# Feed-forward loops of a two-layer transformer block: each engine's order written out by unit of work

## The chip, the cores and the metric

The kernel runs on one core of one Trainium2 chip. A core has TensorE (PE in the profile, with PEld for its weight loads), VectorE (DVE), ScalarE (ACT), GpSimd (POOL) and SyncE (SP), which work through queues of their own and wait for one another by semaphores. Matmuls write to PSUM, which has 8 banks of 128 partitions x 512 fp32 words; everything else lies in SBUF. The metric is the device time of one execution in microseconds, lower is better. It was measured three times for the kernel before.

## The reference

A block of two layers over 512 image tokens and 256 context tokens, width 1024, in fp32. Layer 0 mixes the tokens by a gated part and a differential attention, layer 1 by an attention over a window. Each layer ends in a feed-forward, and the final output is normalised. What matters here (FFN_HIDDEN is 2816):

```python
def swiglu(h, w_in, w_out):
    g, u = jnp.split(h @ w_in, 2, axis=-1)
    return (jax.nn.silu(g) * u) @ w_out
...
mod = silu_c @ ada_w[l] + ada_b[l]
...
h = h + g2 * swiglu(modulate(h, norm2_g[l], sh2, sc2), ffn_w_in[l], ffn_w_out[l])
if need_ctx:
    hc = hc + cg2 * swiglu(modulate(hc, norm2_g[l], csh2, csc2), ffn_w_in[l], ffn_w_out[l])
```

`need_ctx` holds in layer 0 alone, so its feed-forward works on 768 tokens and that of layer 1 on 512. `mod` for layer 1 is a product of one vector with a 1024 x 6144 matrix (a second one, with `silu_cc`, for its first two parts).

## The kernel before

**Arithmetic.** Each fp32 product is made of three matmuls on the parts of a split (`mm3`): a value is rounded to fp32r by a cast on ScalarE (the high part), and the rest is a subtraction (the low part); then high x high, high x low and low x high are added up in PSUM. So each weight tile, 128 x 512, takes a cast on ScalarE (L913) and a subtraction on GpSimd or VectorE (L917).

**Feed-forward.** `ffn(l)` runs over 22 hidden tiles f of 128 columns. For one f the raw weights are one load of 1 MB, 128 x 2048: four quarters a11, a12 (gate, first and second half of the 1024 inputs), a21, a22 (up). With tokens in two halves of NH (384 in layer 0, 256 in layer 1) this is a 2 x 2 product of 2 x 2 blocks. The first two tiles (three in layer 1) do it directly, eight block products; those are needed while the second half of the tokens is still being prepared. From then on `product(n, f)` makes seven block products in the manner of Strassen and Winograd, numbered 1 to 7, 12 matmuls each (four of 128 inputs, three each). Four of their weights are sums that VectorE makes from the quarters: 5 = a21 + a22, 6 = that less a11, 3 = a12 less that, 7 = a11 less a21 (L968). 1, 2 and 4 use a11, a12 and a22. The accumulators are two banks (one `wide` tile) for each f: products 1, 6, 7, 4 add up in the first, 5 and 3 in the second, and product 2 has a bank of its own. Between them results are read out: after 1 VectorE adds the copy of product 2 (L996, L997) and ScalarE applies Silu; 6 is copied (L1001); 5 is copied to `u` (L1005); after 3 VectorE adds (L1008) and ScalarE applies Silu; after 7 VectorE adds to `u` (L1012) and multiplies (L1014); after 4 it multiplies again (L1017). As 6, 7 and 4 go on adding into the bank just read, each waits for that read. Then the gated tile `hs` is split into `hh` (L116 on ScalarE, L117 on GpSimd).

**Second layer.** A pair of hidden tiles g = (2g, 2g+1) with one of the 8 output tiles m is an output unit: 6 matmuls of 512 columns and, in layer 0, 6 of 256. Each writes one of three `pb` banks, and VectorE adds it to the residual (L766). Output units of a pair are put among the products of the two following hidden tiles. The order in the program is in strings; a digit is a product, a letter an output unit:

```python
("2156ab37cd4", "2a1b56c3d74", "2a1b56c3de7f4ghij", "2a1b56c3de7f4g")[f % 2 if f < NF - 1 else l + 2]
```

So on even f the order is 2156ab37cd4, on odd f 2a1b56c3d74 (for f = 3 each letter is two units). The letters from e on are units of the last pair of which only the first hidden tile is ready.

**Who orders.** The program is scheduled by the compiler's planner, which orders each engine's instructions by priority (program order) and a simulated time; a later instruction may be put ahead of an earlier one. `issue_after(ins)` makes what is created within it come after `ins` on the same engine, without a wait on the chip. The kernel before uses it at a few places only.

**Buffers.** Split weights: 8 tiles in layer 0 (tags `w` and `wf`), 12 in layer 1. Raw first-layer weights: two tiles, in layer 1 a third in the ring. Raw second-layer weights `rawo`: 128 x 1024, one tile in layer 0, two in layer 1. Sums: the two `t` tiles and `sumsq`. Split gated tiles `hh`: six, for three hidden tiles. All loads go out on SP's queue.

**Modulation of layer 1.** In `ffn(0)` the 48 tiles of `ada1` (128 x 1024) are loaded into two buffers (`ar`, L216) and multiplied with the broadcast vector on VectorE (L222, `junk`), the first 16 of them twice. `more` puts one tile after each of four steps of a hidden tile, from f = 4 on.

## Time and profile before

| | us |
|---|---|
| median of three runs | 1638.63 |
| lowest, highest | 1636.87, 1643.16 |
| the profiled execution, first to last instruction | 1641.9 |
| loop over f = 3 to 21 in `ffn(0)` with its end, about | 458 to 960 |
| the same in `ffn(1)`, about | 1288 to 1626 |

The time of the profiled execution beyond its span is not given by the profile; the span is 3.3 us above the median of the runs. In the rows below a matmul lasts longer than the distance to the next one, as matmuls are pipelined: the pace is read from starts, or from a busy stretch and its count. An entry in square brackets is the time in which the engine was idle before an instruction, and what ended it. In rows by group, the last columns are the busy time, the mean of one in ns, and the idle time before them.

### The profile page before, as it was taken

The page shows a single profiled execution, that of the slowest core. Times are in us where ns is not written, and L with a number is a line of the kernel's source. Part 1 is how long each engine was busy: PE and PEld are TensorE (multiplying, and loading weights), DVE is VectorE, ACT ScalarE, POOL GpSimd, SP SyncE. Part 2 cuts the span into 40 slices and gives each one's busy share as a digit, 9 for nine tenths or more (in the row PEclk, how much of TensorE's full clock was granted, in tenths as well). Part 3 has the DMA queues.
Part 4 walks back from the last instruction along what each step waited for, and adds up shares of the span by engine and source line. Part 5 has one row for each costly group of instructions (what it writes and reads, how often), then busy time and mean ns, then how long its engine had stood idle before and what let it go on. Part 6 is the DMA issues. An engine that isn't in the chain of part 4 may idle for free.

```text
span 1641.9 us, 24642 instructions
## 1 busy us (share of the span) xinstructions
PE 1542.8 (94%) x9547; PEld 1367.1 (83%) x9547; DVE 1073.0 (65%) x1980; ACT 724.5 (44%) x1472; POOL 766.9 (47%) x543
## 2 busy tenths in 40 slices
PE   6999989999999999999999988999989999999996
PEld 4776877899899889998989978777868989898886
DVE  4621788756857788666665585665667857666665
ACT  2423675645533233333333244555664544444443
POOL 0463221062157666666666316532222466675662
PEclk9999989999999999999999999999999999999998
DMA  8744100141223343343432012110233222322201
GB/s 317 298 153 169 40 7 1 65 139 68 76 79 116 105 139 131 105 150 126 142 131 77 27 51 91 52 33 25 74 116 123 65 103 92 101 90 103 90 27 52
DMA packets 47957, 161.98 MB, mean 99 GB/s; under 512 B 5472, under 2 KB 9952, under 8 KB 40160
## 3 DMA queue, kind: packets, MB, share of 16 engines
q1 hardware_dynamic: 47696, 160.28, 28.4%
q8 instruction: 75, 1.23, 0.3%
q14 instruction: 42, 0.34, 0.1%
q10 hardware_dynamic: 144, 0.13, 0.0%
HBM read 158.29 MB, written 2.10 MB: 98 GB/s over the span
## 4 chain that ended last, share of the span: by engine, by line
PE 69%; DVE 11%; POOL 6%; DMA 5%; ACT 4%; issue 3%; POOLq 0%; SPq 0%; DVEq 0%; ACTq 0%
PE pw L100 9%; PE pw L101 9%; PE pw L102 9%; PE pb L100 7%; PE pb L101 7%; PE pb L102 7%; POOL w L917 5%; DMA raw<-ffn_in 3%; PE pf L100 3%; PE pf L101 2%; PE pf L102 2%; PE pb L1257 2%; PE pb L1246 2%; PE pf L351 2%; DVE t L968 2%
## 5 line engine op out<-in xcount | busy, mean ns | idle before, releaser
L100 PE MATMUL pw<-ax,w 128*128 128x384 f32 (+2 forms) x732 | 237.5, 328 | 16.1 <-DVE q L1012 6.7
L101 PE MATMUL pw<-ax,w 128*128 128x384 f32 (+2 forms) x732 | 237.9, 325 | 4.1 <-DVE ax L458 2.5
L78 POOL TENSOR_TENSOR w<-raw,w 128x512 fp32r<-128x512 f32 (+1 forms) x84 | 127.6, 1526 | 243.2 <-ACT w L75 220.8
L102 PE MATMUL pw<-ax,w 128*128 128x384 f32 (+2 forms) x732 | 236.7, 325 | 2.1 <-POOL w L917 2.1
L917 POOL TENSOR_TENSOR w<-raw,w 128x512 fp32r<-128x512 f32 x119 | 177.7, 1507 | 54.2 <-ACT w L913 53.4
L917 POOL TENSOR_TENSOR w<-t,w 128x512 fp32r<-128x512 f32 x90 | 133.4, 1482 | 139.9 <-ACT w L913 136.5
L100 PE MATMUL pb<-hh,w 128*128 128x512 f32 x480 | 167.3, 362 | 12.8 <-ACT hh L116 8.3
L766 DVE SCALAR_TENSOR_TENSOR xT<-pb,mod,xT 128x512 f32<-128x512 f32 (+3 forms) x208 | 144.5, 704 | 43.8 <-PE pb L102 43.1
L101 PE MATMUL pb<-hh,w 128*128 128x512 f32 x480 | 171.2, 358 | 0.5 <-POOL hh L117 0.5
L102 PE MATMUL pb<-hh,w 128*128 128x512 f32 x480 | 170.7, 357 | 0.0
L100 PEld LDWEIGHTS pw<-ax,w 128*128 128x128 f32 x732 | 142.0, 195 | 27.2 <-DVE q L1012 8.1
L100 PE MATMUL pw<-T,w 128*128 128x384 f32 (+1 forms) x508 | 159.1, 314 | 4.8 <-DVE hs L1008 2.4
L101 PE MATMUL pw<-T,w 128*128 128x384 f32 (+1 forms) x508 | 158.6, 312 | 4.0 <-DVE T L117 4.0
L102 PE MATMUL pw<-T,w 128*128 128x384 f32 (+1 forms) x508 | 158.2, 312 | 0.0
L101 PEld LDWEIGHTS pw<-ax,w 128*128 128x128 f32 x732 | 142.6, 195 | 12.1 <-DVE ax L458 3.4
L102 PEld LDWEIGHTS pw<-ax,w 128*128 128x128 f32 x732 | 142.4, 195 | 6.0 <-POOL w L917 2.7
L913 ACT CAST w<-t 128x512 fp32r<-128x512 f32 x104 | 64.5, 621 | 176.8 <-DVE t L968 122.5
L917 POOL TENSOR_TENSOR w<-rawo,w 128x512 fp32r<-128x512 f32 x63 | 94.1, 1493 | 66.5 <-ACT w L913 66.5
L100 PEld LDWEIGHTS pb<-hh,w 128*128 128x128 f32 x480 | 89.5, 189 | 27.0 <-ACT hh L116 10.8
L100 PEld LDWEIGHTS pw<-T,w 128*128 128x128 f32 x508 | 97.2, 192 | 9.7 <-DVE hs L1008 3.9
L101 PEld LDWEIGHTS pw<-T,w 128*128 128x128 f32 x508 | 97.4, 192 | 6.6 <-DVE T L117 4.6
L102 PEld LDWEIGHTS pb<-hh,w 128*128 128x128 f32 x480 | 90.3, 188 | 13.1
(363 smaller groups left out, 4056.7 us busy)
## 6 DMA issues: line engine op xcount, KB each, us to landing
raw<-ffn_in SPq DMA_DIRECT2D x44, 1024.0 KB, 4.9
ar<-ada SPq DMA_DIRECT2D x24, 1024.0 KB, 7.3
ar<-ada SPq DMA_DIRECT2D x48, 512.0 KB, 3.5
rawo<-ffn_out SPq DMA_DIRECT2D x44, 512.0 KB, 3.9
raw<-odd_out SPq DMA_DIRECT2D x32, 256.0 KB, 2.7
raw<-qk SPq DMA_DIRECT2D x16, 256.0 KB, 7.9
raw<-uv SPq DMA_DIRECT2D x16, 256.0 KB, 2.7
raw<-even_out SPq DMA_DIRECT2D x8, 512.0 KB, 4.2
```

The lines of the kernel that those rows point to most:

```text
L78: eng.tensor_tensor(lo, raw, hi.bitcast(F32), ALU.subtract)
L100: mm(out, s[0], m[0], start=start, stop=False, **kw)
L101: mm(out, s[0], m[1], start=False, stop=False, **kw)
L102: return mm(out, s[1], m[0], start=False, stop=stop, **kw)
L351: nc.tensor.matmul(ps[32 * q:32 * q + 32, :w], cst[:, k, :], t[:, w * q:w * q + w], start=k == 0, stop=k == KT - 1, skip_group_check=True)
L766: self.nc.vector.scalar_tensor_tensor(h, ps[:, r], self.modcol(l, j, m, who), h, ALU.mult, ALU.add)
L913: nc.scalar.copy(t[:, 0, :], src)
L917: eng.tensor_tensor(t[:, 1, :], src, t[:, 0, :].bitcast(F32), ALU.subtract)
L968: nc.vector.tensor_tensor(t, x, y, how)
L1246: last = nc.tensor.transpose(pt[:, x * P:(x + 1) * P], es[2 * (x % 2) + x // 2][:, kb * P:(kb + 1) * P], self.ident)
L1257: nc.tensor.matmul(po[64 * h:64 * h + 64, :], V[vb][:, 64 * g:64 * g + 64], t[:, h * TC:h * TC + TC], start=kb == 0, stop=kb == nb - 1, sk ...
```

## The change

In `ffn` each engine's instructions of the loop are chained in the written order (`run`, one chain each for PE, DVE, ACT, POOL and SP). The order is a list of units; weights are prepared by a list of jobs in the order of their use, 8 (layer 0) or 12 (layer 1) ahead of the units. An output unit stands between most products: 215s6s3s7s4 for every f from 4 on. Each product pair of accumulators becomes two single banks out of four; for that the wide PSUM tiles move to a pool of their own, which is released and opened again around the feed-forwards. Product 2 uses the `fill` bank and is copied at once. Second-layer weights are loaded in tiles of 128 x 512, two in layer 0 and six in layer 1. The modulation tiles are loaded from ScalarE's queue, three for each hidden tile from f = 3 on, and their dots have three fixed places, after products 1 and 7 and after the second output unit. All low parts of weights go to GpSimd, but for one of two second-layer tiles in layer 1. The direct tiles and everything outside the feed-forwards keep their work. The diff, cut to its core:

```diff
     def wide(self):
-        return self.pp.tile([P, 1024], F32, name=self.uid("pw"), tag="w", bufs=2)
+        return self.wp.tile([P, 1024], F32, name=self.uid("pw"), tag="w", bufs=2)
+    def single(self):
+        return self.wp.tile([P, 512], F32, name=self.uid("pw"), tag="s", bufs=4)
+    def open_wide(self):
+        self.wp = self.tc.alloc_tile_pool(name=self.uid("wide"), bufs=1, space=bass.MemoryType.PSUM)
...
         self.close_ring()
+        self.wp.release()
+        self.open_wide()
...
+        tail, tiles = {}, []
+        def run(key, fn, *args, **kw):
+            with tc.issue_after(tail[key].ins) if key in tail else ExitStack():
+                tail[key] = fn(*args, **kw)
+            return tail[key]
+        def add(key, out, x, y, how):
+            return run(key, {"DVE": nc.vector, "POOL": nc.gpsimd}[key].tensor_tensor, out, x, y, how)
+        def ada_load():
+            if todo:
                 ll, j, k = todo.pop(0)
-                t = self.ada_tile(ll, j, k)
+                t = self.adap.tile([P, D], F32, name=self.uid("ar"), tag="ar", bufs=self.ada_bufs)
+                r = (j * KT + k) * P
+                run("ACT", nc.scalar.dma_start, t, a["ada1"][r:r + P, :])
+                tiles.append((ll, j, k, t))
+        def ada_dots():
+            if tiles:
+                ll, j, k, t = tiles.pop(0)
                 for who in range(2 if j < 2 else 1):
-                    self.ada_dot(ll, j, k, t, who)
+                    run("DVE", self.ada_dot, ll, j, k, t, who)
...
+        nrawo = (2, 6)[l]
+        halves = [(g, h) for g in range(NF // 2) for h in range(4)]
+        def load():
+            if halves:
+                g, h = halves.pop(0)
+                t = ring.tile([P, 512], F32, name=self.uid("rawo"), tag="rawo", bufs=nrawo)
+                run("SP", nc.sync.dma_start, t, a["ffn_out"][l, g, :, h * 512:h * 512 + 512])
+                outs.append(t)
...
-                w_ = self.wide()
-                state[f] = [w_[:, :NH], w_[:, 512:512 + NH]]
+                state[f] = [self.single()[:, :NH] for _ in range(2)]
...
+            for k in range(len(W)):
+                run("PE", self.mm3, ps, W[k], A[k], k == 0, k == len(W) - 1)
+            run("DVE", self.residual, l, 5, m, off, n, ps)
...
+            for v in ("2ss1s5s6s3s7s4s" if f == 3 else "215s6s3s7s4" if f < NF - 1 else
+                      ("215s6s3s7sef4ghij", "215s6s3s7sef4g")[l]):
+                if v.isdigit():
+                    units.append((int(v), f))
+                    jobs.append((int(v), f))
+                elif v == "s":
+                    g, m = todo_m.pop(0)
+                    units.append(("s", g, m))
+                    if m % 2 == 0:
+                        jobs.append(("s", g, m))
                 else:
-                    m = "efghijkl".index(v)
-                    Wl.append(s2_weights(NF // 2 - 1, m))
-                    for off, n in whos:
-                        s2_part((NF - 2,), m, Wl[m][:1], off, n)
-        ahead = len(Wl)
-        for m in range(ahead, KT):
-            Wl.append(s2_weights(NF // 2 - 1, m))
+                    units.append(("t", "efghij".index(v)))
+        jobs += [("b", m) for m in range(0, KT, 2)]
+        R = (8, 12)[l]
+        Wt, Wl, sumt = {}, [], []
+        def sum_tile():
+            self.ns += 1
+            sumt.append(self.sumsq()[:, :512] if self.ns % 3 == 2 else self.tmp("t"))
+            return sumt[-1]
+        self.ns = 0
+        ahead_raw = (2, 3)[l]
...
+        def sums(j):
+            n, f = j
+            if n in (5, 6, 3, 7):
+                r = raws[f]
+                a11, a12, a21, a22 = [r[:, i * 512:(i + 1) * 512] for i in range(4)]
+                old = sumt[-1] if sumt else None
+                x, y, how = {5: (a21, a22, ALU.add), 6: (old, a11, ALU.subtract), 3: (a12, old, ALU.subtract),
+                             7: (a11, a21, ALU.subtract)}[n]
+                due[j] = sum_tile()
+                add("DVE", due[j], x, y, how)
+        due, late = {}, []
+        def job():
+            if late:
+                add("DVE", *late.pop())
+            if len(jobs) > 1 and jobs[1][0] not in ("s", "b"):
+                sums(jobs[1])
+            if not jobs:
+                return
+            j = jobs.pop(0)
+            if j[0] == "s":
+                t = Wt[j] = wtile()
+                prepare(outs.pop(0), t, l == 1 and j[2] % 4 == 2)
+                load()
+            elif j[0] == "b":
+                m = j[1]
+                if m % 4 == 0:
+                    f = NF + m // 4
+                    pool = ring if l and f % 3 == 2 else self.Rf
+                    self.big = pool.tile([P, 2048], F32R, name=self.uid("raw"), tag="raw", bufs=1 if pool is ring else 2)
+                t = self.big[:, m % 4 * 512:m % 4 * 512 + 1024].rearrange("p (a b) -> p a b", a=2)
+                prepare(outs.pop(0), t)
+                load()
+                Wl.extend(pieces(t, i) for i in (m, m + 1))
+            else:
+                n, f = j
+                i = {1: 0, 2: 1, 4: 3}.get(n)
+                t = Wt[j] = wtile()
+                prepare(due.pop(j) if i is None else raws[f][:, i * 512:(i + 1) * 512], t)
+                if n == 4:
+                    del raws[f]
+                    if f + ahead_raw < NF:
+                        with tc.issue_after(tail["SP"].ins):
+                            raws[f + ahead_raw] = raw(f + ahead_raw)
+                        tail["SP"] = self.last_raw
+        def prepare(src, t, dve=False):
+            run("ACT", nc.scalar.copy, t[:, 0, :], src)
+            lo = t[:, 1, :], src, t[:, 0, :].bitcast(F32), ALU.subtract
+            if dve:
+                late.append(lo)
+            else:
+                add("POOL", *lo)
...
+            if n == 2:
+                out = st["p2"] = self.fill()[:, :NH]
+                g = st["g"] = self.gated_tile(ring if own else None)
+            elif n == 1:
+                st["w"] = [self.single()[:, :NH] for _ in range(2)]
+                out = st["w"][0]
+            else:
+                out = st["w"][n in (5, 3)]
+            for j in range(4):
+                c = slice(j * P, (j + 1) * P)
+                run("PE", self.mm3, out, (w[:, 0, c], w[:, 1, c]), op[n][j], j == 0 and n in (1, 2, 5), j == 3)
+            g = st["g"]
+            A, B = g[:, :NH], g[:, NH:]
+            ps0, ps1 = st.get("w", (None, None))
+            if n == 2:
+                run("ACT", nc.scalar.copy, A, out)
+            elif n == 1:
+                add("DVE", A, A, ps0, ALU.add)
+                run("ACT", nc.scalar.activation, A, A, AF.Silu)
+                ada_dots()
+            elif n == 6:
+                run("ACT", nc.scalar.copy, B, ps0)
+            elif n == 5:
+                st["u"] = ring.tile([P, NH], F32, name=self.uid("u"), tag="u", bufs=1) if own else self.tmp()[:, :NH]
+                run("ACT", nc.scalar.copy, st["u"], ps1)
+            elif n == 3:
+                add("DVE", B, B, ps1, ALU.add)
+                run("ACT", nc.scalar.activation, B, B, AF.Silu)
+            elif n == 7:
+                add("DVE", st["u"], st["u"], ps0, ALU.add)
+                add("DVE", B, B, st["u"], ALU.mult)
+                ada_dots()
+            else:
+                add("DVE", A, A, ps0, ALU.mult)
+                hi, lo = self.hidden(F32R), self.hidden(F32R)
+                parts = [slice(0, T)] if f < NF - 1 else [slice(NH, T), slice(0, NH)]
+                for c in parts:
+                    run("ACT", nc.scalar.copy, hi[:, c], g[:, c])
+                    add("POOL" if f < NF - 1 else "DVE", lo[:, c], g[:, c], hi[:, c].bitcast(F32), ALU.subtract)
+                hid.append((hi, lo))
+                del state[f]
...
+        with tc.issue_after(self.last_w.ins):
+            for f in range(3, 3 + ahead_raw):
+                raws[f] = raw(f)
+            for _ in range(nrawo):
+                load()
+        for _ in range(R):
+            job()
+        for u in units:
+            if u[0] == "s":
+                g, m = u[1:]
+                for off, n in whos:
+                    s2_part((2 * g, 2 * g + 1), m, pieces(Wt[("s", g, m // 2 * 2)], m), off, n, True)
+                if m % 4 == 1:
+                    ada_dots()
+                if m % 4 in (0, 2, 3) and (m < 4 or g):
+                    ada_load()
+                if m % 2 == 0:
+                    continue
+            elif u[0] == "t":
+                m = u[1]
+                for off, n in whos:
+                    s2_part((NF - 2,), m, Wl[m][:1], off, n, True)
+            else:
+                unit(*u)
+            job()
+        ahead = sum(u[0] == "t" for u in units)
+        while jobs:
+            job()
```

More of the change, by code (lines that the diff above doesn't have):

```diff
@@ L969, in weights @@
             return slot({1: a11, 2: a12, 4: a22}.get(n) if n in (1, 2, 4) else sums[f])
-        def more(n, f, ins):
-            if todo and n in (1, 3, 6, 7) and f >= 4:
-                with tc.issue_after(ins.ins):
-                    ada_some(1)
         def product(n, f):
@@ L1311, in final_rows @@
         dg = self.dg[:, off:off + n]
-        r = self.rstd_rows(sq[:, off:off + n], n, 1.0 / D, self.wide, dg, more, self.bank if off else self.fill)
+        r = self.rstd_rows(sq[:, off:off + n], n, 1.0 / D, self.single, dg, more, self.bank if off else self.fill)
         rs = self.p0.tile([P, 512], F32, name=self.uid("rs"), tag="tq"[off > 0], bufs=2)[:, :n]
```

67 lines of the change are left out of this document (24 added, 43 removed).

## The prediction

> **What bounds the kernel now.** I read the page first, then busy time by stretches, then who TensorE waited for in the two feed-forward loops, then the order of time around two of the waits.
>
> ```profile
> span 1641.9 us, 24642 instructions
> ...
> PE 1542.8 (94%) x9547; PEld 1367.1 (83%) x9547; DVE 1073.0 (65%) x1980; ACT 724.5 (44%) x1472; POOL 766.9 (47%) x543
> ...
> PE 69%; DVE 11%; POOL 6%; DMA 5%; ACT 4%; issue 3%; POOLq 0%; SPq 0%; DVEq 0%; ACTq 0%
> ```
>
> TensorE is busy 94% of the span, so no reordering can bring much; but the chain that ended last is only 69% TensorE. The stretches of the two loops (columns: stretch, its length, then busy us of PE, PEld, DVE, ACT, POOL with counts, granted clock, DMA share, GB/s):
>
> ```profile
> 458.00:960.00 502.00, 485.76 (x2739) 454.94 (x2738) 343.52 (x514) 170.41 (x309) 304.15 (x196) 0.99 0.33 110
> 1266.00:1626.00 360.00, 342.54 (x2325) 316.85 (x2326) 239.91 (x375) 163.13 (x350) 212.36 (x155) 0.98 0.23 77
> 520.00:580.00 60.00, 56.39 (x305) 52.79 (x303) 47.67 (x68) 18.91 (x34) 39.23 (x23) 0.94 0.37 124
> 580.00:630.00 50.00, 47.05 (x260) 43.35 (x261) 42.73 (x57) 16.56 (x31) 32.03 (x20) 1.00 0.37 117
> 630.00:680.00 50.00, 50.00 (x286) 47.12 (x285) 38.12 (x59) 18.59 (x34) 36.91 (x24) 1.00 0.42 141
> 1430.00:1465.00 35.00, 35.00 (x239) 32.42 (x238) 25.39 (x37) 16.07 (x34) 25.03 (x18) 1.00 0.35 121
> ```
>
> Undisturbed, a matmul of loop 0 takes 50.00/286 = 0.175 us and one of loop 1 35.00/239 = 0.146 us. A hidden tile has 84 product matmuls and 48 (loop 1: 24) for the second layer: 132 x 0.175 = 23.1 us and 108 x 0.146 = 15.8 us. Where TensorE did wait, in 470 to 946 us and in 1298 to 1616 us (total, times, longest):
>
> ```profile
> PE pb L100 <- ACT hh L116: 8.3, 6, 2.9
> PE pb L100 <- ACT hs L996: 4.1, 4, 1.6
> PE pw L100 <- ACT hs L1001: 1.8, 1, 1.8
> PE pb L100 <- DVE ctxT L766: 1.2, 2, 0.8
> ```
> ```profile
> PE pw L100 <- DVE q L1012: 6.7, 4, 2.5
> PE pw L100 <- DVE u L1012: 4.7, 2, 2.4
> PE pw L100 <- DVE hs L1008: 2.4, 4, 0.8
> PE pw L100 <- ACT u L1005: 0.8, 1, 0.8
> ```
>
> That is 8.3 + 4.1 + 1.8 + 1.2 = 15.4 us in loop 0 and 6.7 + 4.7 + 2.4 + 0.8 = 14.6 us in loop 1. Their cause shows in the order of time, once in each loop:
>
> ```profile
> 753.38 0.34 PE L102 MATMUL pw<-T,w 128*128 128x384 f32 x1
> 753.99 0.69 DVE L968 TENSOR_TENSOR t<-raw 128x512 f32<-128x512 f32 x1 [2.77 <-DMA raw<-ffn_in]
> 754.60 0.55 DVE L1017 TENSOR_TENSOR hs<-hs,pw 128x384 f32<-128x384 f32 x1
> 755.17 0.83 ACT L116 CAST hh<-hs 128x768 fp32r<-128x768 f32 x1 [2.89 <-DVE hs L1017]
> 756.06 0.50 PE L100 MATMUL pb<-hh,w 128*128 128x512 f32 x1 [2.35 <-ACT hh L116]
> ```
> ```profile
> 1348.60 0.28 PE L102 MATMUL pw<-T,w 128*128 128x256 f32 x1
> 1350.17 0.69 DVE L968 TENSOR_TENSOR t<-raw 128x512 f32<-128x512 f32 x1 [5.15 <-DMA raw<-ffn_in]
> 1350.78 0.41 DVE L1012 TENSOR_TENSOR u<-u,pw 128x256 f32<-128x256 f32 x1
> 1351.24 0.39 PE L100 MATMUL pw<-ax,w 128*128 128x256 f32 x1 [2.36 <-DVE u L1012]
> ```
>
> VectorE's order holds a weight sum of a later hidden tile (L968) ahead of a PSUM read that TensorE needs (L1017, L1012). The sum sits until its raw weights land, VectorE idle 2.77 and 5.15 us before it, and the read, the cast and TensorE stand behind it. The load had gone out only 7.5 us before the sum ran (1350.17 - 1342.64):
>
> ```profile
> 1342.64 0.33 SPq L804 DMA_DIRECT2D raw<-ffn_in  x1
> ```
>
> **The change, part by part.** *Raw weights and sums.* Sums become jobs in the order of use, 8 or 12 tiles ahead and no further; the next raw load goes out when the last quarter (a22) of a tile has been split. A hidden tile has nine jobs. In loop 0, eight ahead, the job of a22 of f is called after unit 2 of f, and the first sum of f+2, which needs the load that this job lets out, after unit 5 of f+1: one hidden tile and two units later, 23.1 + 2 x 2.1 = 27 us. In loop 1 it is 20 jobs, 20/9 x 15.8 = 35 us. Against 7.5 us for the load the wait shown above has no place left; what stands ahead of VectorE's PSUM reads is ready work.
>
> *Spacing.* Before, product 4 followed product 7 directly on odd tiles, though 4 accumulates into the bank that L1012 reads. Now an output unit stands between. Its price in loop 1 by three rows (a product starts, then an output unit, then the next product):
>
> ```profile
> 1363.48 0.28 PE L100 MATMUL pb<-ax,w 128*128 128x256 f32 x1
> ...
> 1364.91 0.39 PE L100 MATMUL pb<-hh,w 128*128 128x512 f32 x1
> ...
> 1366.31 0.28 PE L100 MATMUL pw<-ax,w 128*128 128x256 f32 x1
> ```
>
> A product is 1.43 us, an output unit 1.40 us; in loop 0 both are 12 matmuls, 2.1 us. The read takes 0.41 us (0.55 in loop 0), so 1.40 us cover it, unless something of over 1 us stands ahead on VectorE. The other reads have two to three units. The gated tile now has three products of cover (6.3 us, 4.3 us) between product 4 and the first output unit that needs it, against multiply, cast and POOL's split. Durations in the loops (busy, mean ns; first loop 0, then 580 to 630 us, then loop 1):
>
> ```profile
> L917 POOL TENSOR_TENSOR w<-t,w 128x512 fp32r<-128x512 f32 x51 | 79.6, 1561 | 76.4 <-ACT w L913 76.3
> L117 POOL TENSOR_TENSOR hh<-hs,hh 128x768 fp32r<-128x768 f32 x19 | 36.4, 1917 | 5.3 <-ACT hh L116 5.1
> L1014 DVE TENSOR_TENSOR hs<-hs,q 128x384 f32<-128x384 f32 x13 | 17.4, 1341 | 0.1
> ```
> ```profile
> L222 DVE SCALAR_TENSOR_TENSOR junk<-ar,cb 128x1024 bf16<-128x1024 f32 x12 | 19.7, 1644 | 0.1
> ```
> ```profile
> L917 POOL TENSOR_TENSOR w<-t,w 128x512 fp32r<-128x512 f32 x37 | 51.2, 1384 | 55.5 <-ACT w L913 55.5
> L117 POOL TENSOR_TENSOR hh<-hs,hh 128x512 fp32r<-128x512 f32 x18 | 28.7, 1595 | 0.4 <-ACT hh L116 0.3
> L968 DVE TENSOR_TENSOR t<-raw,t 128x512 f32<-128x512 f32 x12 | 17.9, 1495 | 3.2 <-POOL w L917 3.2
> L1014 DVE TENSOR_TENSOR hs<-hs,q 128x256 f32<-128x256 f32 x13 | 8.2, 635 | 0.3
> ```
>
> In loop 0: 0.55 + 0.83 + 1.92 = 3.3 us plus one weight split of POOL ahead, 1.56, is 4.9 of 6.3 us. In loop 1, with the longer cast of loop 0 for want of a row: 0.41 + 0.83 + 1.60 + 1.38 = 4.2 of 4.3 us: covered, by little.
>
> *The modulation dots* go from four tiles per hidden tile to three, behind the reads. From 580 to 630 us VectorE worked 42.7 us, 19.7 of them on 12 dots: 23.0 of other work in 50 us, 10.6 per hidden tile. With six dots (the first 16 tiles use two each) a hidden tile now costs 10.6 + 6 x 1.64 = 20.4 of 23.1 us, later 15.5. The first 5.3 hidden tiles are tight: gated tiles late behind a pair of dots (3.3 us more than the 4.9, so 8.2 against 6.3) cost about 1.9 us on each of three even tiles, which start the output units of a new pair. I leave 4 us of waits in loop 0 for that (0 if the dots fall into idle time, 10 if every tile pays 1.9 us), and 1.5 us in loop 1 (0 to 11, below).
>
> *Modulation loads on ScalarE's queue.* The one DMA issued there now:
>
> ```profile
> L303 ACTq DMA_DIRECT2D q<-lqk x1: 389/389/389, 50.7 to 50.7; - x1
> ```
>
> Three per hidden tile are 1.2 us of ScalarE, which is idle for two thirds of loop 0: nothing. Behind a load that had to wait for its buffer would stand the weight casts, 8 tiles ahead of use; the buffer's last dot is over a unit past by then. SP loses these 48 issues and queues only raw and rawo.
>
> *PSUM.* Four single banks instead of two pairs: two hidden tiles in flight as before. Product 2 takes the fill bank and is copied at once, so it no longer holds one of the three output banks until L996: the 4.1 us of that row go. Pools reopened in PSUM wait at most for residuals that are past or covered by the other products: nothing, 2 us at most.
>
> *POOL in loop 1* gives VectorE only one split in nine: 8 x 1.38 + 1.60 = 12.7 of 15.8 us. Hidden while it stays ahead by 12 tiles.
>
> *The clock.* 0.94 over 520 to 580 us, where the longest wait (2.9 us) lies, but 1.00 over 630 to 680 and 1430 to 1465, which have none. The loops' 0.99 and 0.98 make about 5 + 7 = 12 us lost. I credit 5 of them, by rounding and because some waits stay. The Trainium skill (TensorE: Matmul & The Clock Gate, HAM oscillation) says that the clock falls only after idle gaps of some 3.4 us; by that rule none of these waits would cost any clock, the credit would be 0 and the forecast 5 us later. The 0.94 beside a longest wait of 2.9 us speaks against it here.
>
> **Sum.** Loop 0: 15.4 - 4 = 11.4. Loop 1: 14.6 - 1.5 = 13.1. Clock 5. Together 29.5 us: 1641.9 - 29.5 = 1612.4 of span. The runs' median 1638.6 lies 3.3 us below the profiled span, so 1609.
>
> **Rivals.** *All waits and the whole clock loss go:* 15.4 + 14.6 + 12 = 42 us, 1597. For it: stretches without any wait exist already. Against: VectorE at 20.4 of 23.1 us.
>
> *The waits only shrink:* a sum held up by POOL takes 1.50 us (the L968 row of loop 1); if it stands before L1012, product 4 waits 1.50 + 0.41 - 1.40 = 0.5 us on each of 19 tiles, 10 us, and 6 us more come in the dot stretch, with the clock credit of 5 kept at 2: 1609 + 10 + 6 + 3 = 1628.
>
> *POOL and VectorE exclude each other, and that becomes the pace.* The stretched rows speak for it (all splits of second-layer weights, ns least/median/most):
>
> ```profile
> L917 POOL TENSOR_TENSOR w<-rawo,w x63: 1276/1297/2858, 447.6 to 1586.7; 128x512 fp32r<-128x512 f32 x63
> ```
>
> A split of 1.30 us in the median takes 1.56 in the mean of loop 0, and L968 goes from 0.69 to 1.50. If two-input work on SBUF ran strictly one after another at these means, loop 1 would need 12.7 + 4 x 0.69 + 0.69 + 0.64 = 16.8 us per hidden tile, loop 0 9 x 1.56 + 1.92 + 4 x 0.69 + 1.34 + 6 x 1.64 = 29.9 us with six dots and 25.0 with three. Over 20.1 tiles' worth of matmuls (19 x 84 for products, 88 x 12 for outputs, over 132) loop 0 takes 5.3 x 29.9 + 14.8 x 25.0 = 528 us against 502 now, loop 1 20.1 x 16.8 = 338 against 343 now (360 less 17 for the 144 matmuls of 0.12 us that precede it): 26 - 5 = 21 us slower, 1660. It decides once these sums exceed what a tile takes now, 25.0 (502/20.1) and 17.1 us (343/20.1). Against it: the means already hold the waiting, so it is counted twice; with 1.30 and 0.69 loop 1 needs 9 x 1.30 + 5 x 0.69 + 0.64 = 15.8, level with its matmuls. The Trainium skill (SBUF — State Buffer, Who interferes with whom) has this as a rule: a VectorE operation with two SBUF inputs and a GpSimd operation that reads SBUF block each other for the whole instruction. By that rule this rival is the forecast wherever the sums exceed the matmuls; the trace agrees that both stretch, not that nothing overlaps.
>
> **Numbers.** Forecast 1609, 0.53; all waits gone 1597, 0.15; shrunk 1628, 0.18; exclusion 1660, 0.14. Half a per cent of 1638.6 is 8 us, what a measurement here can tell from no change. Faster, below 1630: 0.53 + 0.15 + 0.08 of the shrunk = 0.76; same 0.10; slower 0.14. The range runs from 1594 (all waits gone, less 3) to 1640; above it lies the exclusion alone.
>
> **What would show it.** Right: no VectorE wait for raw<-ffn_in within the loops; L1012 and L996 gone from TensorE's waits; clock 1.00 in 520 to 580. Wrong: TensorE waiting for POOL's w or hh, hidden tiles of over 23.5 or 16.3 us without a wait for a DMA, or VectorE waiting for ar.

## The result, and the profile after

Median 1605.57 us (1603.73 to 1606.12, four runs) against 1640.89 us for the kernel before in the same series (1636.87 to 1646.36, four runs): ratio 0.977, interval 0.975 to 0.980. The profiled execution spans 1601.9 us, 40.0 less than before. The forecast of 1609 is 3.4 us too high; the cause that it gave for the waits holds for a part of them alone.

The page of the changed kernel, the lines that were shown of before:

```profile
span 1601.9 us, 24950 instructions
...
PE 1524.8 (95%) x9547; PEld 1354.8 (85%) x9547; DVE 1076.4 (67%) x1949; ACT 722.9 (45%) x1472; POOL 846.9 (53%) x574
...
PE 79%; DVE 13%; ACT 3%; issue 3%; DMA 1%; POOL 0%; SPq 0%; POOLq 0%; DVEq 0%; ACTq 0%
```

The chain that ended last is now 79% TensorE (before 69%). What TensorE waited for in 380 to 960 us, without the rows that lie ahead of the loop or behind it, then in 1220 to 1600 us (total, times, longest; a row behind the loop is left out):

```profile
PE pb L106 <- DVE xT L774: 5.9, 7, 1.9
...
PE pw L106 <- DVE q L879: 1.2, 1, 1.2
...
PE pb L107 <- POOL hh L879: 0.7, 1, 0.7
PE pw L106 <- DVE u L879: 0.6, 1, 0.6
```
```profile
PE pb L107 <- POOL hh L123: 2.8, 2, 2.1
PE pb L106 <- ACT hh L122: 2.5, 1, 2.5
```

L106 to L108 are the old L100 to L102, L774 the old residual L766, L122 and L123 the old split L116 and L117; most operations of the loops now carry the line of the helper, L879. Loop 0 keeps 8.4 us of waits (before 16.1, with two rows of 0.5 and 0.2 us that the prediction left out), all but 0.7 us between 475 and 618 us. Loop 1 keeps 5.3 us at its very start (hh, 1262 to 1270 us) and none from 1270 to 1574.

Where the time came from is best read by stretches. In equal windows of the two loops, before first, then after (columns as in the prediction):

```profile
460.00:940.00 480.00, 464.10 (x2600) 435.25 (x2599) 326.20 (x478) 160.78 (x290) 300.68 (x193) 0.99 0.34 113
...
1290.00:1570.00 280.00, 268.16 (x1802) 247.37 (x1801) 184.66 (x261) 121.43 (x251) 183.41 (x130) 0.99 0.27 93
```
```profile
460.00:940.00 480.00, 471.45 (x2677) 443.43 (x2676) 353.01 (x501) 162.86 (x301) 321.29 (x196) 1.00 0.36 115
...
1290.00:1570.00 280.00, 280.00 (x1935) 260.94 (x1934) 170.79 (x246) 130.20 (x264) 238.34 (x157) 1.00 0.27 86
```

TensorE's idle time falls from 480 - 464.10 = 15.9 to 8.6 us and from 11.8 to 0: 19.2 us. Its busy time per matmul falls as well, from 464.10/2600 = 0.1785 to 0.1761 us and from 0.1488 to 0.1447: times 2677 and 1935 matmuls 6.4 + 7.9 = 14.3 us (an estimate, as the mix of matmuls in a window is nearly, not exactly, the same). About half of that is the clock: in stretches of 20 us the granted clock of these windows was 0.91 or 0.92 five times before and 0.91 once after, else 1.00, which makes 8.8 and 1.8 us lost, a gain of 7. The other half is not explained. (By the mean clock of the whole span, 0.977 before and 0.986 after, the gain is 0.023 x 1641.9 - 0.014 x 1601.9 = 15 us; some 8 of them lie outside the two windows.)

### The profile page after: what moved, and what is told of

It reads as the page before. It is cut to its first block, busy times and chain, and to the rows that moved or that the text cites. A ratio compares the mean times of both kernels' runs of the same rounds, so it can differ in the third digit from the quotient of the medians.

```text
span 1601.9 us, 24950 instructions
## 1 busy us (share of the span) xinstructions
PE 1524.8 (95%) x9547; PEld 1354.8 (85%) x9547; DVE 1076.4 (67%) x1949; ACT 722.9 (45%) x1472; POOL 846.9 (53%) x574
## 4 chain that ended last, share of the span: by engine, by line
PE 79%; DVE 13%; ACT 3%; issue 3%; DMA 1%; POOL 0%; SPq 0%; POOLq 0%; DVEq 0%; ACTq 0%
PE pw L106 11%; PE pw L107 11%; PE pw L108 10%; PE pb L107 8%; PE pb L106 8%; PE pb L108 8%; PE pf L106 4%; PE pf L107 4%; PE pf L108 4%; DVE junk L228 3%; PE pb L1408 2%; PE pb L1397 2%; PE pf L359 2%; PE pw L1360 1%; DMA ar<-ada 1%
## 5 line engine op out<-in xcount | busy, mean ns | idle before, releaser
L106 PE MATMUL pw<-ax,w 128*128 128x384 f32 (+2 forms) x732 | 233.9, 323 | 4.4 <-ACT ax L200 1.6
L107 PE MATMUL pw<-ax,w 128*128 128x384 f32 (+2 forms) x732 | 234.7, 321 | 2.0 <-DVE ax L466 1.4
L108 PE MATMUL pw<-ax,w 128*128 128x384 f32 (+2 forms) x732 | 233.7, 320 | 1.4 <-DVE w L944 1.4
L774 DVE SCALAR_TENSOR_TENSOR xT<-pb,mod,xT 128x512 f32<-128x512 f32 (+3 forms) x208 | 145.8, 706 | 118.2 <-PE pb L108 118.0
L879 POOL TENSOR_TENSOR w<-raw,w 128x512 fp32r<-128x512 f32 x114 | 179.6, 1590 | 39.6 <-ACT w L879 39.4
L879 POOL TENSOR_TENSOR w<-t,w 128x512 fp32r<-128x512 f32 x102 | 157.1, 1544 | 60.9 <-ACT w L879 60.9
L106 PE MATMUL pb<-hh,w 128*128 128x512 f32 x480 | 172.5, 359 | 7.8 <-DVE xT L774 5.2
L107 PE MATMUL pb<-hh,w 128*128 128x512 f32 x480 | 172.4, 359 | 3.5 <-POOL hh L123 2.8
L108 PE MATMUL pb<-hh,w 128*128 128x512 f32 x480 | 172.2, 359 | 0.0
L107 PE MATMUL pw<-T,w 128*128 128x384 f32 (+1 forms) x508 | 157.1, 310 | 1.2 <-DVE T L123 1.2
L108 PE MATMUL pw<-T,w 128*128 128x384 f32 (+1 forms) x508 | 157.1, 310 | 0.0
L106 PE MATMUL pw<-T,w 128*128 128x384 f32 (+1 forms) x508 | 156.4, 310 | 0.0
L106 PEld LDWEIGHTS pw<-ax,w 128*128 128x128 f32 x732 | 139.1, 191 | 12.9 <-ACT ax L200 2.4
L107 PEld LDWEIGHTS pw<-ax,w 128*128 128x128 f32 x732 | 139.4, 191 | 10.2 <-DVE ax L466 3.1
L106 PE MATMUL pf<-ax,w 128*128 128x256 f32 (+2 forms) x420 | 139.9, 333 | 8.3 <-DVE qf L252 5.5
L108 PEld LDWEIGHTS pw<-ax,w 128*128 128x128 f32 x732 | 139.4, 191 | 4.1 <-DVE w L944 1.7
L108 PE MATMUL pf<-ax,w 128*128 128x256 f32 (+2 forms) x420 | 138.8, 330 | 0.0
L107 PE MATMUL pf<-ax,w 128*128 128x256 f32 (+2 forms) x420 | 138.8, 330 | 0.0
L228 DVE SCALAR_TENSOR_TENSOR junk<-ar,cb 128x1024 bf16<-128x1024 f32 x64 | 111.1, 1735 | 8.7 <-DMA ar<-ada 8.1
L879 POOL TENSOR_TENSOR w<-rawo,w 128x512 fp32r<-128x512 f32 x60 | 108.9, 1816 | 11.9 <-ACT w L879 11.9
L879 DVE TENSOR_TENSOR hs<-hs,pw 128x384 f32<-128x384 f32 (+1 forms) x114 | 55.2, 484 | 87.3 <-PE pw L108 74.8
```

The source lines that it names most:

```text
L106: mm(out, s[0], m[0], start=start, stop=False, **kw)
L107: mm(out, s[0], m[1], start=False, stop=False, **kw)
L108: return mm(out, s[1], m[0], start=False, stop=stop, **kw)
L228: return self.nc.vector.scalar_tensor_tensor(junk, t, 1.0, self.cb[who], ALU.mult, ALU.mult, accum_out=self.acc[who][:, col:col + 1])
L774: ins = self.nc.vector.scalar_tensor_tensor(h, ps[:, r], self.modcol(l, j, m, who), h, ALU.mult, ALU.add)
L879: tail[key] = fn(*args, **kw)
```

## The experiments

Each run stands against the kernel before on the same chip. For the stages I read four starts on TensorE in each trace: the first output unit of layer 0 (`pb<-hh`), the first squares with ones behind loop 0 (`pf<-ones,sq`), the first output unit of layer 1, and the squares with ones behind loop 1.

| kernel | median us | ratio, interval | loop 0 | loop 1 |
|---|---|---|---|---|
| before | 1640.9 to 1643.1 | 1 | 493.1 | 330.3 |
| the change | 1605.6 | 0.977 (0.975 to 0.980) | 474.3 | 315.1 |
| e1 no written order | 1631.2 | 0.994 (0.993 to 0.996) | 511.5 | 314.8 |
| e2 VectorE's order alone | 1600.2 | 0.976 (0.972 to 0.979) | 478.4 | 314.6 |
| e3 written, old order of units | 1655.0 | 1.010 (1.007 to 1.013) | 513.0 | 323.0 |
| e4 before, sums later | 1638.1 | 0.998 (0.997 to 1.000) | 494.4 | 323.8 |
| e5 neither written nor spaced | 1629.4 | 0.993 (0.990 to 0.995) | 511.1 | 314.7 |
| e6 pairs of banks | 1666.0 | 1.015 (1.012 to 1.018) | 515.1 | 330.4 |
| e7 weights 4 ahead | 1618.0 | 0.986 (0.983 to 0.989) | 478.1 | 327.2 |
| e8 second dots left out | 1595.5 | 0.972 (0.969 to 0.975) | 462.3 | 316.1 |
| e9 before, single banks | 1611.6 | 0.981 (0.979 to 0.984) | 475.2 | 313.2 |
| e10 7 next to 4 | 1637.6 | 0.997 (0.996 to 0.999) | 487.3 | 329.9 |
| e11 e2 and another first tile | 1598.7 | 0.974 (0.972 to 0.977) | 478.5 | 314.2 |
| e12 e11 and dots spread | 1597.2 | 0.973 (0.970 to 0.975) | 472.8 | 314.3 |

In e1, e2, e5, e11 and e12 the first output unit of layer 0 starts some 10 us earlier (447 to 452 us against 459 to 463), so that loop 0 looks that much longer there.

**e1: the change without any chain.**

```diff
-            with tc.issue_after(tail[key].ins) if key in tail else ExitStack():
+            with ExitStack():
                 tail[key] = fn(*args, **kw)
```

> The changed kernel with its order of units, jobs and loads in the program, but without the chains: the planner is free again to move instructions past one another. Theory A (what counted was that VectorE no longer holds a sum that waits for its raw weights ahead of a PSUM read; loads and jobs placed early in the program give most of that by themselves): 1605 to 1618 us, with few waits of VectorE for raw<-ffn_in. Rival B (the written order is what keeps the sums back): the planner puts the sums ahead again, waits of VectorE for raw<-ffn_in of 15 us and more in the loops, and a time near the kernel before, 1625 to 1640 us.

**e2: of the five chains only VectorE's.** The condition becomes `key == "DVE" and key in tail`.

> The changed kernel with VectorE's chain alone, the four others left to the planner. Theory A: the order of VectorE was the cause, so this comes within 5 us of the changed kernel, 1603 to 1611 us. Rival B (TensorE's order of units counts by itself, as the planner interleaves products and output units matmul by matmul): 1615 to 1630 us.

**e3: all chains, but the order of units of before.**

```diff
-    "2ss1s5s6s3s7s4s" if f == 3 else "215s6s3s7s4" if f < NF - 1 else
-    ("215s6s3s7sef4ghij", "215s6s3s7sef4g")[l]
+    "2ss1ss56ss3ss74" if f == 3 else ("2156ss37ss4", "2s1s56s3s74")[f % 2] if f < NF - 1 else
+    ("2s1s56s3s7ef4ghij", "2s1s56s3s7ef4g")[l]
```

> The changed kernel, everything chained, with the order of units of the kernel before: 2156ss37ss4 on even tiles, 2s1s56s3s74 on odd ones. Theory A (spacing is of small use once VectorE's reads have only ready work ahead): product 4 behind product 7 waits the read of 0.41 or 0.55 us and its semaphores, some 0.9 us on each of about 18 odd tiles, and the gated tile has one product more of cover: 12 to 20 us slower than the changed kernel, 1618 to 1626 us. Rival B (the spacing removed most of the waits, 2.4 us on each odd tile of loop 1 and as much in loop 0): 1635 us or more.

**e4: the kernel before, its first sum of tile f (L968) ordered behind L1017 of tile f - 2.**

```diff
+                        if n == 5 and f - 2 in s1:
+                            es.enter_context(tc.issue_after(s1[f - 2].ins))
                         nc.vector.tensor_tensor(t, x, y, how)
...
-                self.last_s1 = nc.vector.tensor_tensor(g[:, :NH], g[:, :NH], ps0, ALU.mult)
+                self.last_s1 = s1[f] = nc.vector.tensor_tensor(g[:, :NH], g[:, :NH], ps0, ALU.mult)
```

> The kernel before with one edge in VectorE's order: the first sum of tile f comes after the last multiply (L1017) of tile f-2. Nothing else is changed. Theory A (sums ahead of PSUM reads, waiting for raw weights, caused the waits): the waits of TensorE for L1012 go, 10 to 12 us in loop 1, and 5 to 8 us in loop 0 with them: 1618 to 1628 us. Rival B (the waits came from products 7 and 4 standing together): 1636 to 1642 us, with the 2.4 us waits of product 4 still there.

e1 gives 1631 and e2 1600: of the five chains VectorE's is the one that counts, and the intervals of e2 and of the change overlap (e2 lies a little below A's range). e1's time is rival B's, but B's reason isn't there: VectorE waits for `raw<-ffn_in` once, 1.8 us, and TensorE waits all the same, 13.0 us for residuals and 5.4 us for `hs` in 380 to 960 us, none of these after 658 us. e3 is slower than before. Its time too is rival B's (1635 or more), but not by the reads of product 7, which are the second row here (waits of TensorE in 380 to 960 us; a third, for u, has 1.9 us):

```profile
PE pb L106 <- DVE xT L774: 26.5, 12, 5.5
PE pw L106 <- DVE q L879: 4.3, 6, 1.0
```

The first row is what costs: output units wait for a bank until VectorE has added an earlier one to the residual. That the pairs use up the three `pb` banks is how I read it. A written order needs an order of units that leaves room for it: the same chains give 1655 with the one and 1606 with the other.

e4 is the test of the cause that the prediction named, and it does take the late sums away: VectorE's waits for `raw<-ffn_in` fall to a single one of 1.4 us over both loops, from 52.5 (the rows of before are 22.0 and 3.5 in loop 0, 19.9 and 7.1 in loop 1). TensorE's longest rows in 380 to 960 us then are:

```profile
PE pb L100 <- ACT hh L116: 7.6, 5, 2.9
PE pb L100 <- ACT hs L1002: 4.3, 5, 1.5
PE pb L100 <- ACT w L913: 3.9, 3, 1.6
```

Loop 0 is no shorter (494.4), loop 1 by 6.5 us, the kernel by 3 to 5 us: rival B's time, though not its sign, as the waits for L1012's read in loop 1 fall from 11.4 to 4.1 us. The trace of before says the same. In loop 1 five of the six waits for L1012, 10.9 us, stand behind a sum that had waited 4.4 to 5.3 us for its raw weights. In loop 0 this holds for one of the six waits for `hh`, the one that the prediction shows. The longest of them, and two more, stand behind modulation dots (before, VectorE and then TensorE):

```profile
552.50 2.19 DVE L222 SCALAR_TENSOR_TENSOR junk<-ar,cb 128x1024 bf16<-128x1024 f32 x1
...
556.28 0.54 DVE L1017 TENSOR_TENSOR hs<-hs,pw 128x384 f32<-128x384 f32 x1
...
557.74 0.80 PE L100 MATMUL pb<-hh,w 128*128 128x512 f32 x1 [2.86 <-ACT hh L116]
```

The sum that ran between dot and read (1.41 us) had waited 0.25 us. e4 is no clean subtraction either: three waits for a weight's cast (3.9 us, the third row above) are new.

The next four ask what is left then: the fourth corner, the banks, the depth and the dots.

**e5: e1 with e3's order of units.**

> The change with the order of units of before (7 directly followed by 4, output units in pairs) and without any written-out order: the fourth corner beside the change (order written, units spaced: 1605.6), the spaced units alone (1631) and the written order alone (1655). It has what is left of the change: weights 8 or 12 tiles ahead, four single banks, dots at fixed units, raw loads of half tiles. Theory A (spacing and a written order of VectorE pay only together; what else the change has is worth little): 1635 to 1650, about the kernel before, so spacing alone gains some 10 us and the written order alone costs some 10. Theory B (what gains is that the weights are ready far ahead, as predicted, and the order only keeps it): 1615 to 1631, no slower than the spaced units alone. Theory C (the planner's freedom was hiding the pairs): over 1655.

**e6: the change, its accumulators as two pairs of banks.**

```diff
-                st["w"] = [self.single()[:, :NH] for _ in range(2)]
+                w_ = self.wide()
+                st["w"] = [w_[:, :NH], w_[:, 512:512 + NH]]
```

(The same in the direct tiles.)

> The change, but the products write pairs of two banks (two of 1024 columns) in place of four single banks, so that both halves of a pair come free at one time. Theory A (the single banks matter little, since two hidden tiles are in flight either way, and the waits left are for output banks and residuals): 1603 to 1610, PE's waits for pw still under 5 us in loop 0. Theory B (single banks let the next product start while the other half is being read; 48 hidden tiles times some 0.3 us): 1615 to 1630, with new waits of PE's pw for VectorE's u or q.

**e7: weights 4 tiles ahead.** `R = (4, 4)[l]` in place of `(8, 12)[l]`.

> The change with weights 4 tiles ahead in both loops in place of 8 and 12. Theory A (the depth is reserve that is seldom used: VectorE waited for raw weights 1.7 us in all): 1603 to 1615; in loop 1, where GpSimd splits eight of nine jobs and is 82% busy, at most a few waits of TensorE for GpSimd's w. Theory B (the depth carries the gain, as the prediction had it, since a sum that waits for its raw weights stands ahead of the reads of PSUM): VectorE's waits for raw come back to over 10 us, and the time is 1620 to 1640.

**e8: one dot for a modulation tile.**

```diff
                 for who in range(2 if j < 2 else 1):
-                    run("DVE", self.ada_dot, ll, j, k, t, who)
+                    if who == 0:
+                        run("DVE", self.ada_dot, ll, j, k, t, who)
+                        self.acc[1] = self.acc[0]
```

> The change without the second dot of the first 16 modulation tiles: the context's modulation of the second layer takes the sums of the first vector, so 16 of the dots of 1.7 us are left out, all in loop 0. Every wait of TensorE in loop 0 lies in the stretch where two dots stand together on VectorE (475 to 617 us). Theory A (the residual waits behind a pair of dots and a sum, and TensorE for its bank): PE's waits for xT of L774 in loop 0 fall from 5.9 to under 2 us, the time to 1597 to 1602. Theory B (the waits come from GpSimd and VectorE stretching each other, or from anything else in that stretch): the waits stay over 4 us and the time within 2 us of the change.

e5 falls outside theory A and in theory B's range: without chains the order of units changes nothing that shows (1629.4 against 1631.2). B's reason for it, the depth, is e7's question. e7 costs 12 us, nearly all in loop 1 (327.2), where TensorE now waits for GpSimd, 18 times by up to 1.2 us (window 1180 to 1660 us):

```profile
PE pw L108 <- POOL w L879: 5.8, 18, 1.2
```

(Its weight loads wait at 17 further places.) That is A's mechanism (reserve; VectorE waits 2.2 us for raw) with a larger price than A's bound. e8 is 10 us faster than the change, 1.5 us more than A's range, and its wait for xT in loop 0 falls from 5.9 to 0.7 us, as A had it.

e6 is the surprise: 60 us slower than the change and slower than before, when A expected nothing. Its waits of TensorE in loop 0, then one of them in the order of time, and the same place in the changed kernel. The matmul is the first of product 5, into the second accumulator; VectorE's `hs<-hs,pw` reads the first, which product 1 has just filled:

```profile
PE pw L106 <- DVE hs L879: 30.3, 24, 7.9
```
```profile
675.30 0.34 PE L108 MATMUL pw<-ax,w 128*128 128x384 f32 x1
676.35 0.44 PE L106 MATMUL pw<-T,w 128*128 128x384 f32 x1 [0.72 <-DVE hs L879]
...
675.74 0.56 DVE L879 TENSOR_TENSOR hs<-hs,pw 128x384 f32<-128x384 f32 x1 [2.83 <-PE pw L108]
```
```profile
670.51 0.33 PE L108 MATMUL pw<-ax,w 128*128 128x384 f32 x1
670.69 0.33 PE L106 MATMUL pw<-T,w 128*128 128x384 f32 x1
...
670.96 0.56 DVE L879 TENSOR_TENSOR hs<-hs,pw 128x384 f32<-128x384 f32 x1 [2.81 <-PE pw L108]
```

With the pair, product 5 starts at 676.35, when the read of product 1 is over (675.74 + 0.56 = 676.30). With single banks it starts 0.18 us after product 1's last matmul and before that read. No value that 5 needs comes from there: two banks in one tile are guarded as one, and a product waits for a read of the other bank. This trace puts the price at 0.72 us where the read follows at once, 1.9 us where the copy of product 2, which the read adds to, comes late, and once 7.9 us, where two dots stand ahead of the read and the first waits for its load. The Trainium skill (PSUM — Partial Sum Buffer, PSUM bank collisions raise a hardware error) asks for guards by bank. A guard by pair is wider than that.

The last four put this to the kernel before, test the spacing of 7 and 4, and try to beat the change.

**e9: the kernel before with single banks, and nothing else.** The edit of e6 the other way round, with the pool of wide tiles released and reopened around the feed-forwards as in the change.

> The kernel before with one edit: the accumulators of the products are four single banks in place of two pairs. In the changed kernel with pairs, product 5 waited for VectorE's read of product 1 in the other bank of the pair, 0.72 to 1.9 us in nearly every hidden tile, 43 us in all and 60 us of time. Theory A (the coupling costs that only where 5 follows 1 directly or VectorE's order keeps the read back; before has a free order and an output unit between 1 and 5 in every second tile): 1632 to 1643, the waits of PE's pw for hs of L1008 (2.4 us in loop 1) gone and little else. Theory B (single banks alone carry most of the gain): 1605 to 1625.

**e10: 7 next to 4.** "215s6s3s74s" in place of "215s6s3s7s4" (and "2ss1s5s6s3s74ss" for f = 3).

> The change with one edit in the order of units: product 4 follows product 7 directly and the output unit comes after 4, in every hidden tile. Both accumulate into the same bank, so 4 can't start before VectorE has read 7. The prediction took that read as 0.41 us (0.55 in loop 0), covered by an output unit of 1.40 or 2.1 us. Theory A (the spacing of 7 and 4 is what pays of the new order): some 0.7 us a tile over 27 tiles and more where dots and sums stand ahead, with the clock 20 to 35 us: 1625 to 1640, PE's waits for q and u 15 us or more. Theory B (the order of before cost its 50 us by output units in pairs, which run out of the three banks): 1606 to 1615, PE's waits for q and u under 8 us.

**e11: e2, with loop 1's first tile in the order "2156ss3ss7ss4ss".**

> The change with VectorE's order alone written out (1600.2 when run so), and loop 1's first hidden tile in the order 2, 1, 5, 6, output, output, 3 and so on, so that four products stand before the first output unit. In the changed kernel TensorE waits 5.3 us there for the splits of the direct hidden tiles (ACT and POOL hh, 1262 to 1270 us). Theory A: these waits go and nothing takes their place, 1594 to 1598. Theory B (that hole is filled by work that is then missing later, or 1 to 5 to 6 wait for one another in its stead): 1599 to 1602.

**e12: e11 with the dots spread.** One dot at a time, after products 1 and 5, the second output unit and product 7; a modulation tile is loaded when its buffer has been free for two units.

> As the run beside it (VectorE's order alone written out, loop 1's first tile with four products ahead), and with the dots spread: one dot at a place instead of two, at four places of a hidden tile, so that no pair of dots stands ahead of a residual. In loop 0 TensorE's waits lie where two dots stand together (475 to 617 us); without the second dots the change took 1595.5, 10 us less, at two thirds of that work. Theory A (a residual waits because two dots and a sum stand together): half of those 10 us or more come back, 1588 to 1593. Theory B (it is the amount of VectorE's work in that stretch): within 3 us of the run beside it.

e9 decides for the banks: 31 us with that one edit, where the change has 35, and a ratio whose interval touches the change's. Loop 0 takes 475.2 us (the change 474.3) and loop 1 313.2 (315.1). The largest row of TensorE's waits in 458 to 936 us of e9, then VectorE's waits for raw weights in loop 0:

```profile
PE pb L106 <- DVE xT L774: 5.0, 8, 1.7
```
```profile
DVE t L977 <- DMA raw<-ffn_in: 27.9, 12, 5.9
...
DVE sq L977 <- DMA raw<-ffn_in: 14.8, 4, 9.1
```

With 16.6 and 6.6 us in loop 1, VectorE waits for late raw weights 65.9 us, more than before (52.5). TensorE hardly notices: in 458 to 936 us it waits 9.5 us in all, with two waits of 0.56 and 0.69 us right behind such a sum, and 1.8 us in 1280 to 1600 us. With e4 this is a crossed pair: e4 removes the late sums and gains 3 to 5 us, e9 keeps them, removes the coupling of the banks and gains 31. e9's page is a warning too: its chain is 70% TensorE, as before's 69%, at 31 us less. These shares didn't measure what could be gained.

e10 loses 32 us to the one moved output unit. TensorE waits for VectorE's q and u, 12.8 and 5.2 us in 380 to 960 us and 6.2 and 3.1 us in 1180 to 1660 us, as A had it. e11 shifts its wait: the 5.3 us for hh at the start of loop 1 go, and one wait of 5.2 us for `hs` stands there instead. So its 1598.7 is e2 within the intervals, theory B. e12's median is 1.5 us below e11's, within their ranges (1594.8 to 1599.0 and 1598.1 to 1602.2): against theory A, spreading brings little once VectorE's chain stands alone. Beside e8, which leaves work out, e12 is the fastest kernel here, 2.7% faster than before; its interval ends where the change's begins.

## Why the prediction was right, and where it was wrong

*The named cause covers a part.* "VectorE's order holds a weight sum of a later hidden tile (L968) ahead of a PSUM read that TensorE needs" is what the two quoted moments show. The one of loop 1 stands for its loop (10.9 of 14.6 us), the one of loop 0 for itself (2.4 of 15.4 us). Taken away alone (e4) the cause is worth 6.5 us of loop 1 and nothing of loop 0; kept, under single banks (e9), it costs TensorE little that shows. The change removes the late sums as well as the coupling, so its time alone couldn't tell the two apart.

*The step that failed is "PSUM".* "Four single banks instead of two pairs: two hidden tiles in flight as before" counted tiles in flight and not who is guarded together. It gave the edit the 4.1 us of the row L996. Alone it is worth 31 us (e9), within the change 60 (e6). A small part of it stood in the prediction's own rows. L1008 reads product 3 from the second bank; the product that waits for it has the operand T (as 5, 6 and 7 have), so it is 7, which writes the first (before, TensorE's last matmul of 3, the read, the first of 7):

```profile
1609.64 0.28 PE L102 MATMUL pw<-ax,w 128*128 128x256 f32 x1
1610.03 0.42 DVE L1008 TENSOR_TENSOR hs<-hs,pw 128x256 f32<-128x256 f32 x1 [0.78 <-PE pw L102]
...
1610.50 0.39 PE L100 MATMUL pw<-T,w 128*128 128x256 f32 x1 [0.58 <-DVE hs L1008]
```

By their operands the waits for L1001 (product 3, behind the read of 6) and for L1005 (product 6, behind the read of 5) are of this kind too: 2.4 + 1.8 + 0.8 = 5.0 of the 30.0 us. The rest of the 31 us has no such name in the list. That the planner moves other work into the coupled places, so that what is left as a wait bears another name, would explain it, but is not shown.

*"Raw weights and sums"*: VectorE's waits for raw went, down to 1.7 us, as forecast; in loop 0 it just wasn't what TensorE waited for. The depth is worth 12 us (e7), because GpSimd's splits need the reserve, as the step "POOL in loop 1" hinted with "hidden while it stays ahead by 12 tiles". With 12 ahead TensorE has no wait in loop 1 behind its start, at 85% busy time of GpSimd (238.34 of 280 us).

*"Spacing"* was right in mechanism, "so 1.40 us cover it": e10 takes the cover away and pays 32 us. As a gain over before it is open. In loop 1 of before the planner ran 36 matmuls with the operand T, three products, and then one with ax right behind them, eight times (1290 to 1600 us), and four of the five long waits of product 4 for L1012 follow such a place; e4 has one such place, e9 and e1 none. So edits of VectorE's order or of the banks changed TensorE's order too, and without chains the strings are worth nothing that shows (e1, e5).

*"The modulation dots"* stayed tight where forecast, in the stretch of two dots per tile, at a place that was not: not the gated tile but the residual behind a dot and a sum, and with it an output bank. After, VectorE and then TensorE:

```profile
578.04 2.20 DVE L228 SCALAR_TENSOR_TENSOR junk<-ar,cb 128x1024 bf16<-128x1024 f32 x1
580.17 0.08 DVE L228 DVE_READ_ACCUMULATOR junk<-ar,cb 128x1 f32 x1
580.17 1.75 DVE L879 TENSOR_TENSOR t<-raw 128x512 f32<-128x512 f32 x1
581.84 0.74 DVE L774 SCALAR_TENSOR_TENSOR xT<-pb,mod,xT 128x512 f32<-128x512 f32 x1
...
582.64 0.39 PE L106 MATMUL pb<-hh,w 128*128 128x256 f32 x1 [1.91 <-DVE xT L774]
```

The 4 us left in loop 0 for it were 8.4, and e8 puts the stretch's whole price at 10.

*The sum* asks how much waiting goes, not which edit takes it. That it came so near with a cause that covers a part is partly luck. Waits: 24.5 forecast to go, 19.2 in the two windows above. Clock: 5 credited, 7 found there. Two gains were no term: the unexplained half of the 14.3 us above, and the stretch between the loops, 8.0 us shorter (329.6 against 337.6), while the first output unit of layer 0 comes 2.1 us later. Of the 8.0 us, 5.6 lie between the last matmul of layer 1's attention (`pb<-ident,pt`) and the first output unit, 72.0 us before and 66.4 after. e1, e2, e3 and e5 have this too (67 to 68), e4 and e9 don't (72) and e6 hardly (70.7). So it needs no chains, and single banks alone don't bring it; which part does was not tried.

*What would show it.* The clock in 520 to 580 us is 1.00, as asked. Of the signs that were to show an error, three appeared in small: VectorE waited for ar (8.1 us in 380 to 960 us; a wait of 0.47 us of TensorE at 475.8 us stands behind one), TensorE waited for GpSimd's hh (0.7 and 2.8 us), and four hidden tiles between 519 and 620 us took 24.1 to 26.8 us, from product 2 to product 2. After 620 us a hidden tile takes 23.07 us and in loop 1 15.6 us, as "23.1 us" and "15.8 us" had it.

*The rivals.* Single operations of GpSimd and VectorE are stretched as before (GpSimd's split `w<-t` 1544 ns in the mean) without becoming the pace: the hidden tiles' 23.07 and 15.6 us stand against the 25.0 and 16.8 of that rival, and with two dots 24.1 to 26.8 against 29.9. "All waits gone" gave 1597, a time that e12 reaches (1597.2).

*Still open:* in e9 the planner also orders TensorE's products anew, as the eight places above show. Whether the 31 us are the coupled waits themselves or the better order that it finds without them isn't separated. Nor was VectorE's chain tried on e9. Nor is it shown why, under the planner, the rest of the change makes loop 0 end 24 us later than e9 does (e1 960.5 us, e9 936.4), which VectorE's chain then takes back.

## What to carry to other kernels

Give each accumulator that is read on its own a tile of its own in PSUM: two banks in one tile are guarded as one, and a list of waits may show little of it. A cause read from two moments of a trace is a hypothesis: count for how many rows of the list it holds (here nearly all of one row in loop 1, one wait in loop 0), and look whether the wait that it starts with (here VectorE's for raw weights) follows the time from kernel to kernel. An order written out by hand is worth only what its spacing allows: here the same chains gave -35 or +12 us by the order of the units, and for the gain one chain of the five was enough.

## What the runs showed of the hardware

Short waits cost clock too, in steps. Stretches of 20 us (columns as above; the clock is the number ahead of the last two), for before, the change, e10 and e3:

```profile
540.00:560.00 20.00, 17.14 (x92) 16.36 (x91) 15.75 (x19) 7.05 (x13) 14.56 (x9) 0.92 0.41 144
560.00:580.00 20.00, 19.95 (x106) 18.74 (x104) 15.65 (x25) 4.49 (x8) 9.89 (x6) 0.91 0.30 95
700.00:720.00 20.00, 18.18 (x97) 17.37 (x96) 11.96 (x20) 6.32 (x11) 12.45 (x8) 0.91 0.57 191
```
```profile
580.00:600.00 20.00, 18.09 (x96) 17.06 (x95) 18.04 (x26) 4.11 (x7) 13.56 (x8) 0.91 0.42 132
```
```profile
480.00:500.00 20.00, 16.69 (x87) 15.19 (x86) 15.07 (x22) 3.50 (x7) 8.21 (x6) 0.91 0.20 67
560.00:580.00 20.00, 18.10 (x105) 17.16 (x104) 16.09 (x24) 6.50 (x12) 11.33 (x8) 1.00 0.29 92
```
```profile
620.00:640.00 20.00, 14.53 (x73) 13.46 (x72) 13.54 (x23) 4.18 (x8) 10.37 (x6) 0.83 0.27 85
```

They hold one long wait each: 2.86 us at 557.74 (before, lost over two stretches), 1.82 at 706.42 (before), 1.91 at 582.64 (the change), 3.31 at 492.08 and 1.90 at 569.34 (e10), 5.47 at 626.57 (e3). At 0.91 some 20 x 0.09 = 1.8 us of clock are lost, at 0.83 3.4. So waits of 1.8 to 5.5 us cost 1.8 or 3.4 us more than themselves, with two that cost nothing: the 1.90 us, and 2.35 us at 756.06 (before; the clock is 1.00 from 740 to 780). The length alone doesn't decide it. In e6 the waits of 0.72 us that recur every 24 us left the clock at 1.00 (660 to 940 us). The Trainium skill (TensorE: Matmul & The Clock Gate, HAM oscillation) puts the limit at some 3.4 us of idle time. Here 1.82 and 1.91 us were enough.
